# A streaming encoder layer: part of the last residual moved to GpSimd, and one chunk's inputs loaded at another place

## The chip, the cores and the metric

The kernel runs on one core of a Trainium2 chip. The metric is device time in microseconds (us) of one execution; the kernel before took 3009.01 us (median of 3 runs, 3008.19 to 3012.99). The core's engines have queues of their own: TensorE (PE in the profile; its weight loads are PEld), VectorE (DVE), ScalarE (ACT), GpSimd (POOL) and SyncE (SP), which here only issues transfers (DMA). ScalarE issues the output transfers.

## The reference

One layer of a hybrid encoder, on 2048 prompt tokens and 64 sample tokens of width 1024, in float32:

```
h  = rms_norm(x, g1) * (1 + sc1) + sh1
z  = h @ w_in                       # conv pair | q | k | v | two gates
conv_out = conv_module(...);  attn_out = band_attention(q, k, v) @ w_attn_out
merged = sigmoid(g_conv) * conv_out + sigmoid(g_attn) * attn_out
x  = x + gt1 * (merged @ w_o)
h2 = rms_norm(x, g2) * (1 + sc2) + sh2
gate, up = split(h2 @ w_ffn_in)
y  = x + gt2 * ((silu(gate) * up) @ w_ffn_out)
```

What matters here is the last line, x + gt2 * (...), and the step that makes `merged`.

## The kernel before

The first phase makes the normalised input, the projections, the convolution and the attention, and leaves their results in device memory: c_d (convolution), o_d (attention), g_d (gates). The second phase goes over the tokens in three blocks (CBLOCKS: 0 to 576, 576 to 1344, 1344 to 2112), called block one, two and three here; the variable s is 0, 1, 2. Blocks two and three have six tiles of 128 tokens. Each block is done as follows.

**Merge and output projection.** A block has two chunks of tokens. For each chunk, `merge` (line 1641) goes over eight column tiles (ct): weights from w_conv_out and w_attn_out (key "ca"), products `ps<-cin` with the chunk's inputs, which `load_mixed` (line 1090) brings with four transfers, two of c_d and two of o_d; VectorE applies the gate columns (tile tg, `gate_columns`, line 1084), and the sum is split into a high and a low part m. The input tiles of the first chunk and of the second lie in different buffers (tags half0, four buffers, and half1, ten buffers, which other tiles share). Then come the products with w_o (pw), the residual, and the second norm.

**Feed-forward.** `up` makes gate and up products for 22 feature tiles f (ps), and `down` and `down_pair` multiply the hidden tiles with w_ffn_out (pd) and add the results to a sum per token tile, acc. In blocks two and three the last two feature tiles (20, 21) are done by one last call of `down` (line 2049): for each token tile 12 products, into two PSUM banks (one for each half of 512 columns, of a tag with four banks), and then on VectorE for each half: add acc to the products (line 2084), scale with the gate row gt2 (line 2090), add the residual x1 (line 2091). For the very last tile of the program (`final`), the scale and the residual are applied to acc ahead of the products (lines 2059 to 2063), so that afterwards only the products are scaled and acc added. Ahead of that last call, lines 2148 to 2157 load the last two weight slabs, the gate row (gt), the residual rows x1s (x<-x_d, two transfers a tile), and, for the block that follows, two gate columns and the inputs of both chunks.

**Weights.** The class Weights loads each weight slab into a staging buffer (wst, three of them; wup, wfo), and `split` (line 442) turns it into a high part (whi, on ScalarE) and a low part (wlo, on GpSimd or VectorE). At most five slabs are split ahead. Line 459 gives "ca" slabs to GpSimd; line 460 gives one to VectorE instead when, by the planner's own costs, GpSimd's work stands more than BEHIND = 4000 ns beyond TensorE's. These costs are written in `Stream.add` (line 171); one for GpSimd is 60 + 2.25 ns per element. The planner (Stream) adds up such costs as the program is written and runs pending actions, such as freeing a slab and splitting the next, when TensorE's sum has advanced by 500 ns (`spend`, line 200).

**Order.** What is written in the program is not yet the order on an engine. The framework puts the instructions of each engine in order at build time: of those that are ready by its own reckoning, the one written first goes first. So an instruction can be issued far ahead of its written place: the scaling of the last tile's acc (`acc<-acc,gt`) is written behind the fifth tile's work and ran at 2971.20 us, when the first tile's last products had not begun. `tc.issue_after(ins)` keeps what is written inside it behind ins on that engine. All engine instructions carry line 105 in the profile (the recording helper); the transfers carry their own lines: 1095 is load_mixed, 1087 gate_columns, 383 weights, 2154 the residual rows, 2094 the outputs.

Of the kernel before, what the change touches and what calls it, by code (L numbers as in the profile page):

```python
# [8 lines left out]
F32 = mybir.dt.float32  # L9
# [11 lines left out]
T = SEQ + SMP  # L21
# [232 lines left out]
class Weights:  # L254
# [5 lines left out]
    def __init__(self, tc, engines, pool, dram, stream, keys, source, staging, held, kept):  # L260
        self.tc, self.stream = tc, stream
        self.sync, self.act, self.dve, self.gps = engines
        self.pool, self.dram, self.keys, self.source = pool, dram, keys, source
        self.staging, self.held = staging, held
        self.sum_pool, self.sum_d, self.sums, self.hold, self.landed = None, None, {}, 0, {}
        self.room, self.leaving = {"wst": staging - 2, "wup": 0, "wfo": 0}, {"wst": 0, "wup": 0, "wfo": 0}
        times, raws, self.limit, self.pin = {}, {}, 1 << 30, None
        self.wait = True
        self.items, self.users, self.need, self.first, self.stored = [], [], {}, set(), {}
        self.unsaved = set()  # L270

        def item(key):
            self.items.append(key)
            self.users.append(0)
            return len(self.items) - 1

        self.rows = {}
        for i, key in enumerate(keys):
            n = times[key] = times.get(key, 0) + 1
            if key[0] == "dn" and n == 1:  # L280
                for f in (key[1], key[1] + 1):
                    if f not in self.rows:
                        self.rows[f] = item(("fr", f))
                self.need[i] = [self.rows[f] for f in (key[1], key[1] + 1)]
                for j in self.rows_of(key):
                    self.users[j] += 1
            elif key[0] == "up" and n == 1:
                self.first.add(i)
                cs = [c for f, op in key[1:] for c in self.columns_of(f, op)]
                for c in cs:  # L290
                    if c not in raws:
                        raws[c] = item(("fi", c))
                self.need[i] = sorted({raws[c] for c in cs})
                for f, op in key[1:]:
                    for c in self.parts_of(f, op):
                        self.users[raws[c]] += 1
            elif n == 1 or not kept(key) or n == 2 and key[:2] == ("qkv", 0):
                if n == 1 and key[:2] == ("qkv", 0):
                    self.unsaved.add(i)
                self.need[i] = [item(key)]  # L300
                self.users[self.need[i][0]] += 1
        self.raws = raws
        self.again = {key for key, n in times.items() if n > 1 and kept(key)}
        self.loaded, self.ready, self.used, self.freed, self.given = {}, [], 0, 0, 0

        self.extra = {"wup": 1, "wfo": 2}
        self.tags = {"fo": ("wfo", "wup", "wst"), "": ("wst", "wup")}
        self.due = {kind: [] for kind in self.tags}
        for i, key in enumerate(self.items):
            self.due[self.kind(key)].append(i)  # L310
        self.load_on("")
# [130 lines left out]
    def split(self):  # L442
        i = len(self.ready)
        key = self.keys[i]
        its = self.need.get(i, ())
        if i in self.first:
            shape = [P, 4 * len(key) - 4, P]
        elif key[0] == "dn":
            shape = [P, len(DN[key[2]]), 512]
        else:  # L450
            shape = list(self.loaded[its[0]][0].shape) if its else self.stored[key][1]
        hi = self.pool.tile(shape, F32R, tag="whi", name="whi", bufs=self.held)
        lo = self.pool.tile(shape, F32R, tag="wlo", name="wlo", bufs=self.held)
        self.ready.append((hi, lo))
        if not its:
            for t, d in zip((hi, lo), self.stored[key][0]):
                self.sync.dma_start(t.bitcast(F32), d)
            return
        e, name = (self.dve, "dve") if key[0] in ("in", "qkv") or key[0] == "wo" and key[1] % 2 else (self.gps, "pool")
        if name == "pool" and self.sum_pool and self.stream.load["pool"] - self.stream.load["pe"] > BEHIND:  # L460
            e, name = self.dve, "dve"
        if i in self.first:
            parts = [(slice(4 * j, 4 * j + 4), self.operand(f, op)) for j, (f, op) in enumerate(key[1:])]
            self.stream.after("act", "pool")
        elif key[0] == "dn":
            parts = [(slice(j, j + 1), part) for j, part in enumerate(self.down_parts(key))]
            self.stream.after("act", "pool")
        else:
            n = 4 if key[0] == "fi" else shape[1]
            parts = [(slice(j, j + n), self.loaded[its[0]][0][:, j : j + n]) for j in range(0, shape[1], n)]  # L470
        for c, src in parts:
            self.act.activation(hi[:, c], src, AF.Copy)
            self.stream.after(name, "act")
            with self.tc.issue_after(self.pin.ins) if self.pin is not None and name == "dve" else nullcontext():
                e.tensor_tensor(lo[:, c], src, hi[:, c].bitcast(F32), ALU.subtract)
        if i in self.first:
            its = [self.raws[c] for f, op in key[1:] if op[0] == "a" for c in self.parts_of(f, op)]
        elif key[0] == "dn":
            its = self.rows_of(key)
        for j in its:  # L480
            self.drop(j, name)

        def then():
            if key in self.again and key not in self.stored and i not in self.unsaved:
                ds = [self.dram.tile(shape, F32, name="w_d" + "_".join(map(str, key)) + "_" + part) for part in "hl"]
                for t, d in zip((hi, lo), ds):
                    self.sync.dma_start(d, t.bitcast(F32))
                self.stored[key] = ds, shape
            self.presum()

        self.stream.at(self.stream.when(name), then, True)
# [98 lines left out]
def streaming_layer(ctx: ExitStack, tc: tile.TileContext, I, O):  # L590
# [1050 lines left out]
    def merge(c0, c1, src, m, ahead, load):  # L1641
        n = c1 - c0
        for ct in range(KT):
            g = ahead.pop(0)
            if ct == 2 and load:
                load()
            wh, wl = W.get(("ca", ct))
            ps = [
                columns(
                    kts(wh, 4 * j, 4 * j + 4), kts(wl, 4 * j, 4 * j + 4), kts(src[0][j], 0, 4), kts(src[1][j], 0, 4), 0, n  # L1650
                )[:, :n]
                for j in range(2)
            ]
            t = piece("t1", "t1")[:, :n]
            stream.after("dve", "pe")
            dve.scalar_tensor_tensor(t, g[0][:, :n], 1.0, ps[0], ALU.add, ALU.mult)
            dve.scalar_tensor_tensor(ps[1], g[1][:, :n], 1.0, ps[1], ALU.add, ALU.mult)
            W.done()
            if ct + 2 < KT:
                ahead.append(gate_columns(c0, c1, ct + 2))  # L1660
            dve.scalar_tensor_tensor(ps[1], ps[1], 2.0, t, ALU.mult, ALU.add)
            stream.after("act", "dve")
            if c0:
                split(m[0][:, ct, :n], m[1][:, ct, :n], ps[1])
            else:
                split_sample(m[0][:, ct, SMP : SMP + n], m[0][:, ct, :SMP], m[1][:, ct, :n], ps[1])
# [102 lines left out]
    for s, (lo, hi) in enumerate(CBLOCKS):  # L1769
# [279 lines left out]
        def down(fs, ws):  # L2049

            last = fs[-1] == NF - 1
            for i, (t, n) in enumerate(tiles):
                if fs[0] == 0:
                    acc[i] = token_row("acc")
                pss = [ps_g.tile([P, 512], F32, tag="gp", name="pd", bufs=4) for _ in range(2)]
                gt = gt2[int(t < SMP)] if last else None
                final = last and hi == T and i == len(tiles) - 1
                x1 = [x1s[q // 3][:n, q % 3] for q in (2 * i, 2 * i + 1)] if last else None
                if final:
                    for j in range(2):  # L2060
                        dst = acc[i][:n, 512 * j : 512 * j + 512]
                        dve.tensor_tensor(dst, dst, gt[:n, 512 * j : 512 * j + 512], ALU.mult)
# [9 lines left out]
                for j, ps in enumerate(pss):  # L2072
# [1 line left out]
                    dst = acc[i][:n, f]  # L2074
                    m = 2 * n if n == SMP else n
                    both = acc[i][:m, f]
                    stream.after("dve", "pe")
                    if fs[0] == 0:
                        act.activation(both, ps[:m], AF.Copy)
                    elif not last:  # L2080
# [73 lines left out]
                nc.sync.dma_start(x1s[q // 3][:n, q % 3], x1_d[t : t + n, 512 * j : 512 * j + 512])  # L2154
        if s + 1 < len(CBLOCKS):
            nxt = [gate_columns(*tile_chunks(*CBLOCKS[s + 1])[0], ct) for ct in range(2)]
            srcs = [load_mixed(*c, i) for i, c in enumerate(tile_chunks(*CBLOCKS[s + 1]))]
        down(list(range(end, NF)), ws)
        stream.flush()

# [28 lines left out]
```

## Time and profile before

| | |
|---|---|
| Median of 3 runs | 3009.01 us |
| Profiled execution | 3009.85 us |
| Its span, first to last instruction | 3008.0 us |
| Mean granted TensorE clock | 0.987 |
| TensorE busy | 2919.7 us, 97% |
| VectorE busy | 2029.9 us, 67% |
| GpSimd busy | 915.9 us, 30% |

A row of the timeline gives the start in us from the span's start, the duration (of a merged group, from its first start to its last end), the engine, the line, the operation, out<-in by tile names, the shapes, the count, and in brackets the engine's idle time just before, with what ended it. In a row of windows stand, for each engine, busy us and the number of instructions, then the granted clock, the DMA engines' busy share, and GB/s. The chain of waits follows the work that ended last back through what released it.

### The profile page before, as it was taken

To read this page: it belongs to the slowest core of one execution; us is meant where nothing else is said; L and a number is where in the kernel's file an instruction comes from. 1 tells how busy PE (TensorE), PEld (TensorE's weight loads), DVE (VectorE), ACT (ScalarE), POOL (GpSimd) and SP (SyncE) were. 2 spreads that over 40 slices of the span, in tenths; PEclk is the share of its full clock that TensorE was granted. 3 is DMA by queue.
4 is the path that set the end of the run, shared out by engine and by line. 5 is a ranking of instruction groups with operands and counts; after the bars stand their busy time and mean duration, and the time that the engine had idled before them with its cause. 6 is when DMAs were issued, how large, how long until landed. Compare 5 with 4: busy or idle time off the path is not lost.

```text
span 3008.0 us, 44650 instructions
## 1 busy us (share of the span) xinstructions
PE 2919.7 (97%) x16199; PEld 2603.0 (87%) x16199; DVE 2029.9 (67%) x3671; ACT 1323.1 (44%) x2375; POOL 915.9 (30%) x575
## 2 busy tenths in 40 slices
PE   7999989999999999989999999999999999999998
PEld 4889867888888788888999999999999898999997
DVE  5887676777867885577777756556666657366567
ACT  3334642563356257464444345434444244333332
POOL 1200210011011102345456432256665341333331
PEclk9999999999999999999999999999999999999999
DMA  9788889878988788886444786446556955355544
GB/s 301 258 295 286 274 262 298 290 249 283 301 266 265 262 251 272 267 285 235 153 153 157 269 266 222 144 140 207 197 175 218 335 194 192 119 169 174 168 161 174
DMA packets 487017, 690.95 MB, mean 230 GB/s; under 512 B 38420, under 2 KB 316808, under 8 KB 486797
## 3 DMA queue, kind: packets, MB, share of 16 engines
q1 hardware_dynamic: 469749, 662.07, 66.8%
q10 hardware_dynamic: 17048, 26.04, 2.4%
q8 instruction: 127, 2.08, 0.3%
q14 instruction: 93, 0.76, 0.1%
HBM read 503.79 MB, written 184.19 MB: 229 GB/s over the span
## 4 chain that ended last, share of the span: by engine, by line
PE 84%; DVE 7%; DMA 5%; issue 1%; ACT 1%; POOL 1%; SPq 0%; ACTq 0%; DVEq 0%; POOLq 0%
PE ps L105 55%; PE pd L105 14%; PE pw L105 6%; PE po L105 2%; PE sc L105 2%; DVE y L105 2%; PE ptp L105 2%; PE pt L105 1%; DMA cin<-o_d 1%; DVE wlo L105 1%; PE pa L105 1%; POOL r L105 1%; DVE pr L105 1%; DMA tg<-g_d 0%; DMA x<-x_d 0%
## 5 line engine op out<-in xcount | busy, mean ns | idle before, releaser
L105 POOL TENSOR_TENSOR wlo<-wst,whi 128x1024 fp32r<-128x1024 f32 (+1 forms) x168 | 384.8, 2294 | 562.8 <-ACT whi L105 500.4
L105 PE MATMUL ps<-t,whi 128*128 128x384 f32 (+1 forms) x2112 | 506.9, 323 | 8.5 <-DVE t L105 6.2
L105 PE MATMUL pd<-whi,hid 128*128 128x512 f32 x1356 | 441.2, 391 | 3.4 <-DVE acc L105 3.4
L105 ACT ACTIVATE whi<-wst 128x1024 fp32r<-128x1024 f32 (+1 forms) x271 | 265.0, 982 | 397.4 <-PE ps L105 132.1
L105 PEld LDWEIGHTS ps<-t,whi 128*128 128x128 f32 x2112 | 370.8, 189 | 17.5 <-DVE t L105 7.4
L105 PE MATMUL ps<-b,whi 128*128 128x384 f32 (+1 forms) x1584 | 379.6, 325 | 4.1 <-DVE pt L105 1.7
L105 DVE SCALAR_TENSOR_TENSOR y<-u,wd,y 128x512 f32<-128x512 f32 (+1 forms) x480 | 367.4, 772 | 6.5
L105 PE MATMUL ps<-hh,whi 128*128 128x512 f32 (+2 forms) x992 | 363.9, 367 | 0.0
L105 PE MATMUL ps<-hh,wlo 128*128 128x512 f32 (+2 forms) x992 | 348.7, 351 | 0.0
L105 PE MATMUL ps<-hl,whi 128*128 128x512 f32 (+2 forms) x992 | 348.3, 351 | 0.0
L105 PE MATMUL ps<-t,wlo 128*128 128x384 f32 (+1 forms) x1056 | 340.9, 323 | 0.0
L105 DVE TENSOR_TENSOR acc<-acc,pd 128x512 f32<-128x512 f32 x440 | 289.8, 683 | 65.8 <-PE pd L105 62.3
L105 PEld LDWEIGHTS pd<-whi,hid 128*128 128x128 f32 x1356 | 254.5, 188 | 58.6 <-DVE acc L105 7.0
L105 PEld LDWEIGHTS ps<-b,whi 128*128 128x128 f32 x1584 | 276.9, 189 | 6.2 <-DVE v L105 2.1
L105 PE MATMUL pd<-wlo,hid 128*128 128x512 f32 x700 | 273.8, 391 | 0.0
L105 PE MATMUL ps<-b,wlo 128*128 128x384 f32 (+1 forms) x792 | 256.4, 324 | 0.0
L105 ACT ACTIVATE pr<-pr,sm 128x640 f32<-128x640 f32 (+3 forms) x272 | 200.9, 747 | 120.8 <-DVE sm L105 118.4
L105 PEld LDWEIGHTS ps<-hh,wlo 128*128 128x128 f32 x992 | 189.6, 191 | 22.2 <-DMA wlo<-w_din_l 0.4
L105 PEld LDWEIGHTS ps<-hh,whi 128*128 128x128 f32 x992 | 190.2, 192 | 19.1 <-issue 1.8
L105 PEld LDWEIGHTS ps<-hl,whi 128*128 128x128 f32 x992 | 190.3, 192 | 16.0 <-issue 1.4
L105 PEld LDWEIGHTS ps<-t,wlo 128*128 128x128 f32 x1056 | 199.3, 189 | 0.9
L105 POOL TENSOR_TENSOR r<-t,mhalf 128x1 f32<-128x1 f32 (+3 forms) x68 | 80.6, 1186 | 381.0 <-DVE t L105 378.2
(218 smaller groups left out, 5652.2 us busy)
## 6 DMA issues: line engine op xcount, KB each, us to landing
whi<-w_din_h SPq DMA_DIRECT2D x72, 512.0 KB, 5.2
wlo<-w_din_l SPq DMA_DIRECT2D x72, 512.0 KB, 6.5
wst<-sum_d SPq DMA_DIRECT2D x132, 256.0 KB, 2.9
wmod<-in_w_ada SPq DMA_DIRECT2D x48, 512.0 KB, 6.9
sum_d<-ws SPq DMA_DIRECT2D x88, 256.0 KB, 2.2
wst<-in_w_ffn_in SPq DMA_DIRECT2D x84, 256.0 KB, 3.2
wst<-in_w_in SPq DMA_DIRECT2D x40, 512.0 KB, 7.6
wst<-in_w_ffn_in SPq DMA_DIRECT2D x37, 512.0 KB, 5.5
```

The lines of the kernel that those rows point to most:

```text
L105: return f(*args, **kw)
```

## The change

In the last `down` call of blocks two and three, the sums acc of the third, fourth and fifth of the six tiles are scaled with gt2 and get their residual x1 on GpSimd, behind the last weight split that was given to GpSimd up to there (W.low), and written ahead of the products. After the products of these tiles VectorE then scales the products and adds acc. The other tiles are left as they were. And of the next block's inputs only those of the first chunk are loaded ahead of that `down` call; those of the second chunk are loaded from within the first chunk's merge, at its seventh column tile (block one keeps its load at the third).

```diff
@@ Weights.split
-                e.tensor_tensor(lo[:, c], src, hi[:, c].bitcast(F32), ALU.subtract)
+                low = e.tensor_tensor(lo[:, c], src, hi[:, c].bitcast(F32), ALU.subtract)
+            self.low = low if name == "pool" else self.low
@@ merge
-            if ct == 2 and load:
+            if ct == (6 if c0 else 2) and load:
                 load()
@@ down
             last = fs[-1] == NF - 1
+            ahead = range(len(tiles) - 4, len(tiles) - 1) if last and s else ()
+            with tc.issue_after(W.low.ins) if ahead else nullcontext():
+                for i, j in [(i, j) for i in ahead for j in range(2)]:
+                    dst = acc[i][:, 512 * j : 512 * j + 512]
+                    gps.tensor_tensor(dst, dst, gt2[0][:, 512 * j : 512 * j + 512], ALU.mult)
+                    gps.tensor_tensor(dst, dst, x1s[(2 * i + j) // 3][:, (2 * i + j) % 3], ALU.add)
...
-                final = last and hi == T and i == len(tiles) - 1
+                final = last and (i in ahead or hi == T and i == len(tiles) - 1)
...
-                if final:
+                if final and i not in ahead:
                     for j in range(2):
...
-                    stream.after("dve", "pe")
+                    stream.after("dve", "pe", *["pool"] * (i in ahead))
@@ ahead of the last down call
-            srcs = [load_mixed(*c, i) for i, c in enumerate(tile_chunks(*CBLOCKS[s + 1]))]
+            srcs = [load_mixed(*tile_chunks(*CBLOCKS[s + 1])[0], 0)]
         down(list(range(end, NF)), ws)
```

More of the change, by code (lines that the diff above doesn't have):

```diff
@@ L266, in __init__ @@
         self.room, self.leaving = {"wst": staging - 2, "wup": 0, "wfo": 0}, {"wst": 0, "wup": 0, "wfo": 0}
-        times, raws, self.limit, self.pin = {}, {}, 1 << 30, None
+        times, raws, self.limit, self.pin, self.low = {}, {}, 1 << 30, None, None
         self.wait = True
```

## The prediction

> **What bounds the kernel now.** I read the page's busy shares and chain first, then the timeline of each engine around the two places that the diff touches: the last down-projection products of a block, and the start of the next block's merge.
>
> ```profile
> PE 2919.7 (97%) x16199; PEld 2603.0 (87%) x16199; DVE 2029.9 (67%) x3671; ACT 1323.1 (44%) x2375; POOL 915.9 (30%) x575
> PE 84%; DVE 7%; DMA 5%; issue 1%; ACT 1%; POOL 1%; SPq 0%; ACTq 0%; DVEq 0%; POOLq 0%
> ```
>
> TensorE is busy nearly everywhere, so only places where it stands still, and the end of the program, can give time. The timeline of block three's end shows VectorE, then a TensorE row that waited:
>
> ```profile
> 2986.99 1.29 DVE L105 TENSOR_TENSOR pd<-pd,acc 128x512 f32<-128x512 f32 x2
> ...
> 2989.39 1.27 DVE L105 TENSOR_TENSOR acc<-pd,x 128x512 f32<-128x512 f32 x2
> 2990.58 1.29 DVE L105 TENSOR_TENSOR pd<-pd,acc 128x512 f32<-128x512 f32 x2
> ...
> 3003.74 1.27 DVE L105 TENSOR_TENSOR acc<-pd,acc 128x512 f32<-128x512 f32 x2
> 2990.12 0.50 PE L105 MATMUL pd<-whi,hid 128*128 128x512 f32 x1 [0.55 <-DVE acc L105]
> ```
>
> VectorE has no gap. A tile is six instructions, started 0.60 us apart: 3.59 us from 2986.99 to 2990.58. TensorE waits for it each time, because each tile needs two of four PSUM banks and the banks come back only with VectorE's last add. The end of the program is VectorE's at 3005.01, and the last output transfer closes the span of 3008.0. Block two has the same shape, and its last wait is the first product of the next merge:
>
> ```profile
> 2344.71 1.38 DVE L105 TENSOR_TENSOR pd<-pd,acc 128x512 f32<-128x512 f32 x2
> 2365.13 1.27 DVE L105 TENSOR_TENSOR acc<-pd,x 128x512 f32<-128x512 f32 x2
> 2362.28 0.62 PE L105 MATMUL ps<-cin,whi 128*128 128x384 f32 x2 [0.55 <-DVE acc L105]
> ```
>
> After it, the chain of waits through the boundary of blocks two and three, the TensorE row at its end, and the windows of the merge products (busy, count, granted clock, DMA share, GB/s):
>
> ```profile
> 2355.51 14.82 DMA cin<-o_d
> 2370.82 4.80 DMA wst<-in_w_attn_out
> 2375.72 0.75 ACT whi L105
> 2376.69 0.48 ACT m L105
> 2377.19 0.57 DVE m L105
> 2377.80 0.62 PE L105 MATMUL ps<-cin,whi 128*128 128x384 f32 x2 [2.55 <-DVE m L105]
> 2362.28:2374.92 12.64, 12.64 (x71) 12.64 (x72) 1.00 1.00 340
> 2374.92:2384.00 9.08, 6.50 (x27) 5.67 (x27) 0.81 1.05 339
> ```
>
> Inputs of the second chunk (cin) stand in SyncE's queue ahead of merge weights; ScalarE has to wait for the weights with the split of m behind it; m's split holds a PSUM bank; TensorE stops. It made 27 products in 9.08 us, where at the earlier pace (12.64 / 71 = 0.178 us) they take 4.8: this place costs 4.3 us, partly idle, partly at a granted clock of 0.81.
>
> **The change, part by part. Block three's tail.** Removed from VectorE: for tiles three to five, the scale and the residual add drop out of the sequence add, scale, add residual for each half; what stays is scale the products, add the sum. That is 2 instructions x 3 tiles = 6, at 0.60 us: 3.6 us, if VectorE goes on setting the pace. TensorE's tile is 2.85 us (2990.12 until its bank wait), VectorE's new tile 4 x 0.60 = 2.39. Followed through: VectorE ends tile three at 2992.97, four at 2995.4, five at 2997.8; TensorE, unstalled, ends tile six near 2998.6, and VectorE needs its second half at 2999.5. So TensorE doesn't take over, and the end moves from 3005.0 to 3001.4. The other bound: where the halves arrive one after another, the two instructions of a half run dependent, 0.74 us apart, as in block one's tail:
>
> ```profile
> 1724.70 0.70 DVE L105 TENSOR_TENSOR pd<-pd,gt 128x512 f32<-128x512 f32 x1
> 1725.43 0.69 DVE L105 TENSOR_TENSOR acc<-pd,x 128x512 f32<-128x512 f32 x1
> ```
>
> Then a tile is 2.94 and the gain 3 x (3.59 - 2.94) = 1.9 us. I take 3.3, near the interleaved end, which is what this stage shows.
>
> **The work added to GpSimd** is 12 instructions per block of a form that the trace has with other operands; its groups:
>
> ```profile
> L105 POOL TENSOR_TENSOR ws<-wfo,ws 128x512 f32<-128x512 f32 x16 | 20.8, 1302 | 4.7 <-DVE x L105 4.0 <-POOL ws L105 0.2
> L105 POOL TENSOR_TENSOR ws<-ws,wup 128x512 f32<-128x512 f32 x8 | 14.4, 1800 | 0.6
> ```
>
> 1.30 us each, 1.80 at worst: 15.6 us a block (21.6). Does it end before VectorE asks? In block three GpSimd is free from 2962.25, the gate row lands at 2971.2, and the second half of tile three gets its last sum late:
>
> ```profile
> 2960.97 1.28 POOL L105 TENSOR_TENSOR wlo<-wst,whi 128x512 fp32r<-128x512 f32 x1 [1.28 <-ACT whi L105]
> 2971.20 1.29 DVE L105 TENSOR_TENSOR acc<-acc,gt 128x512 f32<-128x512 f32 x2 [1.82 <-DMA gt<-gt_d]
> 2981.31 1.27 DVE L105 TENSOR_TENSOR acc<-acc,pd 128x512 f32<-128x512 f32 x2
> ```
>
> Even if GpSimd stands in order at that sum until 2982.6, its ten remaining instructions end at 2995.6, and VectorE wants the last at about 2997.2. Covered by 1.6 us; were it late, VectorE's whole queue, tile six included, would stand behind it.
>
> **Block two's tail.** GpSimd first has weight splits, behind the last of which the new work is ordered:
>
> ```profile
> 2339.52 7.15 POOL L105 TENSOR_TENSOR wlo<-wst,whi 128x1024 fp32r<-128x1024 f32 x3 [11.08 <-DMA x<-x_d]
> 2343.47 0.68 DVE L105 TENSOR_TENSOR acc<-acc,pd 128x512 f32<-128x512 f32 x1
> ```
>
> The third of these splits is written inside the last down call (its buffer comes free only with the last paired product), so after the new work. The planner then has GpSimd 12 x (60 + 2.25 x 512) ns = 14.5 us ahead, over its limit BEHIND of 4 us (line 460), and gives that split to VectorE. So GpSimd starts the new work near 2344.3 and ends by 2360, in time for tile five (adds near 2359 to 2361); but VectorE, which bounds this stage, gets a 128x1024 split that it didn't have:
>
> ```profile
> 2389.45 1.22 DVE L105 TENSOR_TENSOR wlo<-wst,whi 128x1024 fp32r<-128x1024 f32 x1
> 2378.73 2.32 DVE L105 TENSOR_TENSOR wlo<-wst,whi 128x1024 fp32r<-128x1024 f32 x1
> 2375.28 4.68 POOL L105 TENSOR_TENSOR wlo<-wst,whi 128x1024 fp32r<-128x1024 f32 x2 [10.30 <-ACT whi L105]
> ```
>
> 1.22 us alone, 2.32 beside a busy GpSimd. For the first product of the merge the removed instructions of two tiles count (2.4 us, tile three and four; after that TensorE's own 2.85 a tile is the pace): gain 2.4 - 1.2 to 2.4 - 2.3 = 1.2 to 0.1; I take 0.6. Bounds: 2.4 if the split stays on GpSimd, and a loss if GpSimd runs late (below).
>
> On that price, the Trainium skill (SBUF — State Buffer, "SBUF: two separate sides") says that a VectorE instruction with two SBUF inputs and a GpSimd instruction that reads SBUF lock each other out, whichever starts first finishing undisturbed. The row of 2.32 us agrees: it began under the GpSimd pair, which ended at 2379.96, and ran on 1.1 us after that. By the rule alone the split costs 1.22 plus at most one GpSimd instruction, 2.5 us, and block two's gain would be nothing; the instructions that have a PSUM operand would not be touched.
>
> **The moved loads.** Four transfers at each of two boundaries leave their place before the last down call and are written at the seventh column tile of the merge:
>
> ```profile
> 2348.30 1.03 SPq L1095 DMA_DIRECT2D cin<-o_d  x2
> 2351.68 1.08 SPq L1095 DMA_DIRECT2D cin<-c_d  x2
> 2355.51 4.92 SPq L1095 DMA_DIRECT2D cin<-o_d  x2
> 2363.84 0.37 SPq L383 DMA_DIRECT2D wst<-in_w_conv_out  x1
> 2362.74:2366.33 3.59, 3.59 (x22) 3.59 (x22) 3.59 (x8) 0.00 (x0) 2.24 (x1) 1.00 1.06 402
> cin<-o_d SPq DMA_DIRECT2D x4, 768.0 KB, 12.3
> ```
>
> The four from 2351.68 on are those of the second chunk: 3.07 MB, 7.7 us at 402 GB/s. The buffer of the waiting weights came free with the first split (2341.9). Without the four, the weights can go out near 2350 and land before 2363; the last of them landed at 2375.6. The stall of 4.3 us goes; next late are the gate columns, two buffers deep, so I take 4.0. Bounds: 0 and 4.3. The moved transfers are not needed before the second chunk:
>
> ```profile
> 2434.42 0.51 PE L105 MATMUL ps<-cin,whi 128*128 128x384 f32 x2
> ```
>
> Issued at their written place, near 2391, plus the 14.8 us that the slowest took, they land at 2406, 28 us early. At the boundary of blocks one and two the same queue costs little:
>
> ```profile
> 1735.64 0.19 PEld L105 LDWEIGHTS ps<-cin,wlo 128*128 128x128 f32 x1 [0.49 <-POOL wlo L105]
> 1750.76 0.30 PEld L105 LDWEIGHTS ps<-cin,whi 128*128 128x128 f32 x2 [0.68 <-DVE m L105]
> ```
>
> Bounds 0 and 1.2; I take 0.5.
>
> On the stall's size, the Trainium skill (TensorE: Matmul & The Clock Gate, "Part 1") says that the clock falls after an idle window of about 3.4 us. Here it was 0.81 after 2.55 us of idleness. By the rule only the idle part, some 2.6 us, would come back; the row decides for 4.3.
>
> **Sum:** 3.3 + 0.6 + 4.0 + 0.5 = 8.4 us. The profiled execution took 3009.85 us (span 3008.0), so 3001.4 by it; the median of the runs is 3009.01, 0.84 less, which would give 3000.6. I say 3001.0.
>
> **Rivals.** *The loads don't get out of the way.* The program's order is not the issue order: the framework issues what is ready.
>
> ```profile
> 2322.36 0.45 SPq L1095 DMA_DIRECT2D cin<-c_d  x1
> ```
>
> This one, of the first chunk, went out 20 us before its written place. The second chunk's buffers come free at 2340, the weights' at 2341.9; if that order decides, the queue stays as it was and only the tails gain: 3.9, 3005.5. Against it: the transfers that are written earlier go first while the queue is full (share 1.06).
>
> *The stall only moves* to the gate columns or the next weights and half of it stays: 3.9 + 2.2, 3003.3. For it: boundary one already has small waits of this kind.
>
> *GpSimd makes VectorE wait, and it is slower.* If the third split stays ahead on GpSimd, block two's new work starts at 2346.7; at 1.80 us each it ends at 2368.3, VectorE's add of tile five follows, and the first merge product comes near 2369, 6.7 us late. Block three: 2982.6 + 10 x 1.80 = 3000.6, plus 0.7 and tile six's 3.6: no gain. With the stall covered (4.3) and 0.5, the sum is +1.9: 3011.3. It decides from 1.5 us per instruction on. Against it: 1.30 is the mean of most groups, and VectorE's instructions here read PSUM.
>
> *Everything at its good end:* 3.6 + 2.4 + 4.3 + 1.2 = 11.5, 2997.9.
>
> **How the numbers follow.** Forecast 0.56, loads in the way 0.24, stall moves 0.07, GpSimd late 0.06, all good 0.07. This kernel's measurement tells 0.2% (6.0 us) from nothing, so faster is below 3003.0 and slower above 3015.0. Faster: nearly all of the forecast, all good and a little of the moved stall, 0.62. Same: loads in the way and the rests, 0.33. Slower: GpSimd late at its worst, 0.05. The range goes from 2996.5 (just past all good) to 3006.5 (past the loads in the way).
>
> **What would show it.** Block three: from the first down product of the tail to VectorE's last instruction 3.3 us less than before, with four instructions in tiles three to five. Block two: one 128x1024 split on VectorE inside the tail; TensorE waits for the sum shrink. Boundary: weights issued ahead of the second chunk's cin, the granted clock at 1.00 through the merge, no 2.5 us gap. Wrong if cin still stands ahead of the weights, or if VectorE's adds of tiles three to five wait for GpSimd.

## The result, and the profile after

The changed kernel took 3002.89 us (median of nine runs, 2999.85 to 3006.80), the kernel before 3009.92 us in the same comparison (nine runs, 3008.19 to 3016.30). The ratio is 0.9974, 95% interval [0.9966, 0.9983]: 5 to 10 us less. A second comparison gave 0.9973 [0.9963, 0.9983]. The forecast of 3001.0 us was 1.9 us too low and its range held the time.

The profiled execution took 2999.85 us, span 2998.1: the fastest of the nine. Its page, busy time by engine and the chain's shares by engine:

```profile
PE 2914.3 (97%) x16199; PEld 2600.2 (87%) x16199; DVE 2028.5 (68%) x3661; ACT 1323.5 (44%) x2375; POOL 943.0 (31%) x597
PE 83%; DVE 7%; DMA 4%; POOL 2%; issue 2%; ACT 1%; SPq 0%; ACTq 0%; DVEq 0%; POOLq 0%
```

Nothing in these shares says where the 9.9 us between the two spans went; they are read at four places. In the changed kernel's rows load_mixed carries line 1096 and gate_columns 1088, one higher than before. The timeline of the changed kernel at the end of block three (start, duration, engine, operation):

```profile
2965.72 2.40 DVE L105 TENSOR_TENSOR acc<-acc,gt 128x512 f32<-128x512 f32 x2 [2.68 <-DMA gt<-gt_d]
2965.76 7.26 POOL L105 TENSOR_TENSOR acc<-acc,gt 128x512 f32<-128x512 f32 x5 [9.85 <-DMA gt<-gt_d]
...
2972.48 0.56 DVE L105 TENSOR_TENSOR hid<-ps,hid 128x384 fp32r<-128x384 f32 x1 [0.56 <-ACT hid L105]
...
2980.10 3.77 POOL L105 TENSOR_TENSOR acc<-acc,x 128x512 f32<-128x512 f32 x3
2983.77 0.50 PE L105 MATMUL pd<-whi,hid 128*128 128x512 f32 x1 [0.55 <-DVE acc L105]
2984.23 1.29 DVE L105 TENSOR_TENSOR pd<-pd,gt 128x512 f32<-128x512 f32 x2
2985.42 1.28 DVE L105 TENSOR_TENSOR acc<-pd,acc 128x512 f32<-128x512 f32 x2
...
2993.80 1.28 DVE L105 TENSOR_TENSOR acc<-pd,acc 128x512 f32<-128x512 f32 x2
```

The same stretch of the kernel before began with this row:

```profile
2978.84 0.56 DVE L105 TENSOR_TENSOR hid<-ps,hid 128x384 fp32r<-128x384 f32 x1 [0.56 <-ACT hid L105]
```

From the first write of the last pair's hidden tile (2972.48) to VectorE's last instruction (2995.08) it is 22.60 us; before, the same stretch was 26.17 (2978.84 to 3005.01). Tiles three to five now have four VectorE instructions each. GpSimd is through with its sums at 2983.87, before VectorE takes the first of them at 2985.42. From the first tile's products on VectorE still has no gap: it bounds this tail as before, only with six instructions fewer.

The timeline of the changed kernel at the end of block two:

```profile
2338.83 0.56 DVE L105 TENSOR_TENSOR hid<-ps,hid 128x384 fp32r<-128x384 f32 x1 [0.56 <-ACT hid L105]
...
2342.86 4.76 POOL L105 TENSOR_TENSOR acc<-acc,gt 128x512 f32<-128x512 f32 x3
2343.26 1.97 DVE L105 TENSOR_TENSOR wlo<-wst,whi 128x1024 fp32r<-128x1024 f32 x1
...
2352.56 6.30 POOL L105 TENSOR_TENSOR acc<-acc,x 128x512 f32<-128x512 f32 x5
2358.91 0.68 DVE L105 TENSOR_TENSOR acc<-pd,acc 128x512 f32<-128x512 f32 x1
2348.28 0.50 PE L105 MATMUL pd<-whi,hid 128*128 128x512 f32 x1 [1.61 <-DVE acc L105]
2351.86 0.50 PE L105 MATMUL pd<-whi,hid 128*128 128x512 f32 x1 [0.57 <-DVE acc L105]
2360.16 0.52 PE L105 MATMUL ps<-cin,whi 128*128 128x384 f32 x2
```

The kernel before at the same hidden tile:

```profile
2340.23 0.56 DVE L105 TENSOR_TENSOR hid<-ps,hid 128x384 fp32r<-128x384 f32 x1 [0.56 <-ACT hid L105]
```

The third weight split has moved to VectorE, at the head of the tail, and TensorE's first wait for a free bank has grown to 1.61 us. One of 0.57 follows; the later ones are gone, the one ahead of the merge (0.55 before) too. In sum 21.33 us from the hidden tile to the first merge product, 22.05 before (2340.23 to 2362.28). GpSimd's last sum was ready at 2358.86, and VectorE took it at 2358.91: here there was no room to spare.

The timeline of the changed kernel through the boundary of blocks two and three, and its windows there (busy and count for TensorE, its weight loads, VectorE, ScalarE, GpSimd; granted clock, DMA share, GB/s):

```profile
2349.72 0.37 SPq L383 DMA_DIRECT2D wst<-in_w_conv_out  x1
2350.22 0.64 SPq L383 DMA_DIRECT2D wst<-in_w_attn_out  x1
...
2360.54 1.50 SPq L1096 DMA_DIRECT2D cin<-c_d  x2
...
2381.21 0.38 SPq L1096 DMA_DIRECT2D cin<-o_d  x1
2376.22 0.56 DVE L105 SCALAR_TENSOR_TENSOR t<-tg,ps 128x384 f32<-128x384 f32 x1 [3.05 <-DMA tg<-g_d]
2379.56 0.62 PE L105 MATMUL ps<-cin,whi 128*128 128x384 f32 x2 [0.16 <-DVE m L105]
2428.07 0.51 PE L105 MATMUL ps<-cin,whi 128*128 128x384 f32 x2
```

```profile
2360.16:2372.80 12.64, 12.64 (x73) 12.64 (x72) 8.49 (x15) 5.00 (x6) 7.16 (x3) 1.00 1.08 368
2372.80:2384.00 11.20, 11.04 (x63) 10.72 (x62) 6.42 (x12) 4.05 (x5) 2.40 (x1) 1.00 1.04 387
```

The first of the merge weights goes out at 2349.72, 14 us earlier than before (2363.84), and the second chunk's inputs follow behind three pairs of weights. The wait of 2.55 us is gone but for 0.16, the clock stays at 1.00, and from the first merge product to the first product of the second chunk it is 67.91 us, 72.14 before (2362.28 to 2434.42).

What the prediction read as a mean clock of 0.81 is one piece of half clock in the kernel before, right behind the wait; its window:

```profile
2378.40:2381.81 3.41, 3.38 (x12) 2.87 (x11) 3.41 (x4) 1.27 (x2) 1.56 (x1) 0.50 1.02 323
```

Half of 3.41 us is 1.71 us; with the wait of 2.55 us that makes 4.26 (an estimate), the 4.3 us of the stall.

### The profile page after: what moved, and what is told of

It reads as the page before. It is cut to its first block, busy times and chain, and to the rows that moved or that the text cites. A ratio compares the mean times of both kernels' runs of the same rounds, so it can differ in the third digit from the quotient of the medians.

```text
span 2998.1 us, 44671 instructions
## 1 busy us (share of the span) xinstructions
PE 2914.3 (97%) x16199; PEld 2600.2 (87%) x16199; DVE 2028.5 (68%) x3661; ACT 1323.5 (44%) x2375; POOL 943.0 (31%) x597
## 4 chain that ended last, share of the span: by engine, by line
PE 83%; DVE 7%; DMA 4%; POOL 2%; issue 2%; ACT 1%; SPq 0%; ACTq 0%; DVEq 0%; POOLq 0%
PE ps L105 54%; PE pd L105 15%; PE pw L105 6%; DVE y L105 2%; PE sc L105 2%; PE po L105 2%; PE ptp L105 2%; PE pt L105 1%; DVE wlo L105 1%; POOL r L105 1%; PE pa L105 1%; DMA kk<-k_d 1%; DMA whi<-w_din_h 1%; DVE pr L105 1%; DMA bias<-rb_d 0%
```

## The experiments

All kernels are judged by the same four stretches of their profile. "One to two" and "two to three" are the boundaries: from a block's first merge product to the first product of its second chunk. "Tail two" goes from the first hidden tile of the last pair to the next block's first merge product, "tail three" from the first hidden tile of block three's last pair to VectorE's end. Two values are two executions of one kernel. The ratio is that of the timed runs to those of the kernel before in the same comparison.

| kernel | one to two | tail two | two to three | tail three | ratio [95%] |
|---|---|---|---|---|---|
| before | 68.65, 68.68 | 22.05, 22.04 | 72.14, 71.39 | 26.17, 26.17 | 1 |
| changed | 67.50, 67.51 | 21.33, 21.35 | 67.91, 68.26 | 22.60, 22.58 | 0.9974 [0.9966, 0.9983], 0.9973 [0.9963, 0.9983] |
| GpSimd's part alone | 68.82, 71.74 | 21.34, 21.35 | 72.42, 74.29 | 22.59, 22.58 | 0.9998 [0.9986, 1.0009], 1.0002 [0.9993, 1.0012] |
| loads alone | 67.49 | 22.05 | 70.37 | 26.17 | 0.9985 [0.9975, 0.9995] |
| sums in block three only | 69.33 | 22.04 | 67.90 | 22.59 | 0.9969 [0.9958, 0.9981] |
| sums unplanned | 67.49 | 19.63 | 68.93 | 22.59 | 0.9965 [0.9952, 0.9978] |
| loads at the third weight | 70.05 | 21.34 | 67.84 | 22.59 | 0.9975 [0.9965, 0.9986] |
| GpSimd's work doubled | 68.56 | 21.36 | 67.49 | 31.01 | 0.9999 [0.9988, 1.0011] |
| pinned | 68.46, 69.08 | 19.60, 19.61 | 68.93, 71.02 | 22.59, 22.59 | 0.9965 [0.9952, 0.9977], 0.9966 [0.9954, 0.9979] |
| pinned, four tiles | 67.49 | 19.61 | 71.35 | 21.70 | 0.9964 [0.9950, 0.9978] |

The tails repeat to 0.03 us wherever the code is the same. The boundaries don't: up to the tail of block two, the changed kernel and its variants (all but GpSimd's part alone and the loads at the third weight) issue the same instructions in the same order on every engine, and their boundary from one to two still lies anywhere from 67.49 to 69.33. A tail is settled by one profile, a boundary isn't.

Two things account for most of a boundary's extra length: TensorE's waits in it, and whether the clock falls beside them. From two to three the clock fell to 0.50, for 3.41 us each time, in both profiles of the kernel before, in the second of GpSimd's part alone, in the second of the pinned kernel and in pinned with four tiles. The longest wait beside it was 1.78 to 2.98 us. It did not fall in the first profile of GpSimd's part alone, whose waits were 1.42 and 2.98 us. In the ten profiles whose merge weights go out ahead of the second chunk's inputs, the stretch took 67.49 to 71.35 us, 69.0 in the mean; in the four with the inputs ahead, 71.39 to 74.29, 72.6 in the mean.

**GpSimd's part alone.** All eight transfers go back ahead of the last down call.

```diff
-            if ct == (6 if c0 else 2) and load:
+            if ct == 2 and load:
...
-            srcs = [load_mixed(*tile_chunks(*CBLOCKS[s + 1])[0], 0)]
+            srcs = [load_mixed(*c, i) for i, c in enumerate(tile_chunks(*CBLOCKS[s + 1]))]
```

> The GpSimd part alone; both chunks' inputs are loaded at their old place. Theory (two separate gains: VectorE's tails, and the weights' place in SyncE's queue): block three's tail, from the split of the last hidden tile to VectorE's last instruction, is 3.6 us shorter than before, block two's tail gains about 0.7 us, and the gap of about 2.5 us at the fourth column tile of block three's merge, with the granted clock near 0.8, is there again; about 3005.5 us, 4 below before. Rival (the stall went because the third weight split moved to VectorE, not because of the loads): no gap at the fourth column tile, about 3001 us, 8 below before.

The tails came as expected (3.58 and 0.71 us), and the stall stayed. But the time was no better: 3011.36 us beside 3011.94. So it was run again, with the kernel before for a second profile:

> GpSimd's part alone once more: its profile showed 3.58 us less in the tail of block three and 0.71 less in that of block two, while its time showed only 0.6 us (ratio 0.9998, to 0.9986 at best). Theory: the two tails are worth their 4.3 us in every execution, the stall at the boundary is of before's size (72 us for the stretch), and the ratio comes out at 0.998 to 0.9995. Rival: the gain of the tails is real, but with the loads where they were the boundary or the stages ahead of it take it back: the ratio stays at 0.9995 or more, and the profile shows a longer stretch (over 73 us from merge to second chunk) or a longer stage elsewhere.

> A second profile of the kernel before. Theory: the stall at the boundary into block three is there in each execution, 71 to 73 us for the stretch from the first merge product to the first product of the second chunk, with TensorE waits of 2 to 4.5 us for m. Rival: it varies by several us from execution to execution, and the 72.14 of the first profile was a long one: 68 to 70 us here.

The kernel before showed its stall again (71.39 us, 2.02 us of waiting for m). GpSimd's part alone took 3013.24 us, ratio 1.0002: not the expected gain, but what its rival said. The second profile shows part of why: the stretch from merge to second chunk is 74.29 us. Its timeline and a window there:

```profile
2364.59 3.96 SPq L1096 DMA_DIRECT2D cin<-o_d  x2
2372.96 0.37 SPq L383 DMA_DIRECT2D wst<-in_w_conv_out  x1
2381.19 1.06 ACT L105 ACTIVATE whi<-wst 128x1024 fp32r<-128x1024 f32 x1 [12.05 <-DMA wst<-in_w_attn_out]
2383.27 0.62 PE L105 MATMUL ps<-cin,whi 128*128 128x384 f32 x2 [1.84 <-DVE m L105]
2388.64 0.69 PE L105 MATMUL ps<-cin,whi 128*128 128x384 f32 x1 [2.98 <-DVE m L105]
```

```profile
2380.00:2392.00 12.00, 7.18 (x32) 6.53 (x31) 7.89 (x11) 5.48 (x7) 4.71 (x2) 0.86 0.90 273
```

The weights still stand behind the inputs (SyncE issues the first at 2372.96), ScalarE waits 12.05 us for them, and TensorE stands still twice. The time to the second chunk is set by when the weights land, so TensorE, which comes to the merge 0.7 us sooner, waits longer: tail two and boundary together are 93.76 and 95.64 us, before 94.19 and 93.43. The gain in block two is thus not seen in the sum. Block three's 3.58 us are in both profiles; yet the second interval leaves out a gain of more than 2 us. In the second of these executions time also went into stretches whose order of instructions is that of the kernel before: 1730.40 us up to block two's first merge product (1726.99 in the first, 1726.48 and 1728.97 before), and one to two at 71.74. From block two's first merge product to VectorE's end the two took 1275.40 and 1280.01 us, the kernel before 1278.54 and 1277.26. In this part, ahead of the last tail, the clock fell to 0.50 for 3.41 us twice and four times, in the kernel before twice and once. With 1.71 us taken off for each, this part would be 2.8 us shorter than the kernel before's in the mean (an estimate). Whether the rest, and the clock's falls, are scatter or a cost that goes with this kernel, two profiles don't settle; it stays open.

**The loads alone.**

```diff
-            ahead = range(len(tiles) - 4, len(tiles) - 1) if last and s else ()
+            ahead = ()
```

> The moved loads alone; all tails on VectorE as before. Theory: 4 to 5 us less than before, all at the two boundaries (about 1.1 from the first merge product of block two to its second chunk, 4.2 in block three); tails as before, VectorE's last instruction 3.6 us later after the last hidden tile than in the changed kernel; about 3004.5 us. Rival (the gains aren't separate: VectorE's late end of tile six in block two holds the merge's banks anyway): under 2 us less than before, about 3008 us.

The ratio is 0.9985, 4.5 us less [1.5, 7.5]. The tails are those of the kernel before, so all of it comes from the boundaries. From two to three its profile shows 70.37 us:

```profile
2377.95 0.62 PE L105 MATMUL ps<-cin,whi 128*128 128x384 f32 x2 [1.60 <-DVE m L105]
2380.99 0.62 PE L105 MATMUL ps<-cin,whi 128*128 128x384 f32 x2 [0.66 <-DVE m L105]
2366.95 8.81 ACTq L2101 DMA_DIRECT2D out<-acc  x3
2375.87 1.06 ACT L105 ACTIVATE whi<-wst 128x1024 fp32r<-128x1024 f32 x1 [8.87 <-DMA cin<-c_d]
```

That is 1.8 us less than the kernel before, not the expected 4.2. The weights stood ahead here too (SyncE issued the first three pairs from 2353.23 to 2361.44). What ScalarE's split stood behind were three output transfers that ScalarE issues itself; the profile puts their wait down to earlier transfers.

**The sums in block three only.** This differs from the loads alone only in block three's tail.

```diff
-            ahead = range(len(tiles) - 4, len(tiles) - 1) if last and s else ()
+            ahead = range(len(tiles) - 4, len(tiles) - 1) if last and s == 2 else ()
```

> The changed kernel with the GpSimd part in block three only. Theory: block two's tail is as before, the first merge product of block three 0.7 us later against the last hidden tile than in the changed kernel; block three's tail still 3.6 us shorter; no gap at the fourth column tile; about 0.7 us above the changed kernel. Rival (block two's part also carries the gain at the boundary): 3 to 5 us above the changed kernel, with the gap back.

Here the boundary took 67.90 us, without a wait for m. Up to there it is the same order of instructions as in the loads alone, so the 70.37 there was one execution's, and the boundary's gain does not need GpSimd's part in block two. The ratio 0.9969 beside 0.9985 for the loads alone puts block three's tail at 4.8 us (4.0 by the medians), which agrees with the 3.58 of the profile: with the loads out of the way this tail counts. How much of it, the times don't tell, since the two intervals overlap.

**The sums unplanned.** The twelve instructions go to the engine past the planner's books, so that line 460 leaves the third split on GpSimd. In the profile they carry their own lines (2057 and 2058) instead of 105.

```diff
-                    gps.tensor_tensor(dst, dst, gt2[0][:, 512 * j : 512 * j + 512], ALU.mult)
-                    gps.tensor_tensor(dst, dst, x1s[(2 * i + j) // 3][:, (2 * i + j) % 3], ALU.add)
+                    nc.gpsimd.tensor_tensor(dst, dst, gt2[0][:, 512 * j : 512 * j + 512], ALU.mult)
+                    nc.gpsimd.tensor_tensor(dst, dst, x1s[(2 * i + j) // 3][:, (2 * i + j) % 3], ALU.add)
```

> The changed kernel, with the new GpSimd instructions left out of the planner's costs, so that the third weight split of block two's tail stays on GpSimd. Theory (that split on VectorE, 1.97 us, eats most of block two's gain): the first merge product of block three comes 1.2 to 2.0 us earlier against the last hidden tile, nothing else moves by more than 0.5 us; 1 to 2 us less than the changed kernel. Rival (the split was no loss, TensorE is the limit of block two's tail, or GpSimd ends later and VectorE waits): same as the changed kernel within 0.5 us, with VectorE waiting for GpSimd at tile five.

Tail two fell to 19.63 us, 2.42 below the kernel before: what the sums alone are worth there. The split on VectorE therefore costs 21.33 - 19.63 = 1.70 us of it. But GpSimd did make VectorE wait. The timeline:

```profile
2358.14 2.45 POOL L105 TENSOR_TENSOR wlo<-wst,whi 128x1024 fp32r<-128x1024 f32 x1
2360.49 1.33 POOL L2058 TENSOR_TENSOR acc<-acc,x 128x512 f32<-128x512 f32 x1
2361.86 0.69 DVE L105 TENSOR_TENSOR acc<-pd,acc 128x512 f32<-128x512 f32 x1 [2.37 <-POOL acc L2058]
2362.60 0.62 PE L105 MATMUL ps<-cin,whi 128*128 128x384 f32 x2 [0.32 <-DVE acc L105]
2365.59 0.62 PE L105 MATMUL ps<-cin,whi 128*128 128x384 f32 x2 [0.61 <-DVE acc L105]
```

The split slid in ahead of the last residual addition; VectorE stood 2.37 us for that one sum, and TensorE felt 0.93 us of it in the merge (0.32 + 0.61). The ratio, 0.9965, is lower than the changed kernel's 0.9974, with intervals that overlap.

**Pinned.** The same, with later GpSimd splits ordered behind the last sum.

```diff
...
+            behind = self.pin if name == "dve" else self.tail
-            with self.tc.issue_after(self.pin.ins) if self.pin is not None and name == "dve" else nullcontext():
+            with self.tc.issue_after(behind.ins) if behind is not None else nullcontext():
...
-                    nc.gpsimd.tensor_tensor(dst, dst, x1s[(2 * i + j) // 3][:, (2 * i + j) % 3], ALU.add)
+                    W.tail = nc.gpsimd.tensor_tensor(dst, dst, x1s[(2 * i + j) // 3][:, (2 * i + j) % 3], ALU.add)
```

> The twelve sums leave the planner's books and the weight splits that GpSimd issues afterwards stand behind the last of them. Theory: in the kernel without planning, the third weight split slid in ahead of the last residual addition and held VectorE for 2.37 us, which TensorE felt as 0.32 + 0.61 us in the stage that follows; behind the additions it starts 1.3 us later at most, nobody waits for it, and the stage goes back to the changed kernel's 67.9 us while the tail of block two keeps its 19.6 us. In all some 2.6 us under the changed kernel's 67.9 + 21.3, so 0.9 us under the kernel without planning. Rival: the split is the next late: the weights of the merge come 1.3 us later, TensorE waits for a wlo tile for 0.5 to 1.5 us, and nothing is gained on the kernel without planning.

> The pinned kernel once more, since five runs of it left its ratio between 0.9952 and 0.9977. Theory: the tail of block two at 19.6 us again against the changed kernel's 21.3, the boundary into block three between 67.9 and 69 us; median 2999 to 3003 us, ratio 0.996 to 0.997, at or just under the changed kernel's 0.9973. Rival: the low median was a small sample, and the ratio comes out above 0.9973.

> The changed kernel again, beside the variants below. Theory: its gain at the boundary from block two to block three belongs to the order of SyncE's transfers, so the stretch from the first merge product of block three to the first product of its second chunk is again 67.9 us (67.4 to 68.9; before 72.14), and the stretch of the boundary from block one to two is 67.5 us (67.0 to 68.5). Rival: the 67.91 was one lucky execution, and the loads alone are worth what the kernel with the loads alone showed, 70.4 us. Median 3001 to 3004 us, ratio to before 0.9965 to 0.9985.

The changed kernel came out as expected at both boundaries (67.51 and 68.26 us); its median, 3004.14 us, is 0.1 above the expected range. In the pinned kernel the waits for acc in the merge were gone, tail two stayed at 19.6 us, and the split was not the next late. The gate columns were. The second pinned execution:

```profile
2380.24 0.55 DVE L105 SCALAR_TENSOR_TENSOR t<-tg,ps 128x384 f32<-128x384 f32 x1 [4.60 <-DMA tg<-g_d]
2380.94 0.75 PE L105 MATMUL ps<-cin,whi 128*128 128x384 f32 x2 [1.78 <-DVE t L105]
```

Behind this wait the clock fell to 0.50 for 3.41 us. The boundary took 68.93 and 71.02 us, not the expected 67.9 and 67.9 to 69; tail two and boundary together are 88.53 and 90.63 us, in the changed kernel 89.24 and 89.61. So in the profiles the 1.7 us go back to the gate columns, in part or whole. The timed ratios, 0.9965 and 0.9966 (3002.11 us in the second comparison), are lower than the changed kernel's 0.9973 and 0.9974 by some 2.4 us, with intervals that overlap: a better kernel is likely but not shown.

**The loads at the third weight**, in all blocks.

```diff
-            if ct == (6 if c0 else 2) and load:
+            if ct == 2 and load:
```

> The second chunk's four loads are asked for at the third weight in all three blocks, not at the seventh in blocks two and three. SyncE's order then has them ahead of the fourth pair of merge weights at the boundary from block one to two, and at the one from two to three almost where the change has them (two of the four pieces some gate loads earlier, all behind the merge weights). Theory (what counts is that the merge weights stand ahead of the loads, not the written place): the boundary into block three stays at 67.9 us (67.4 to 69), the one into block two gives back part of its 1.15 us and stands at 67.5 to 68.7; the kernel is within 2 us of the changed one. Rival (the written place, four weights later, carries the gain): 70 to 72 us in the boundary into block three, and 3 to 4 us above the changed kernel.

From two to three it was 67.84 us, the changed kernel's value: there SyncE's order has the inputs where the change has them, but for two pieces that go some gate loads earlier. From one to two all four inputs now go ahead of the sixth pair of weights in the trace (which the expectation calls the fourth), and that stretch took 70.05 us, with three waits of TensorE of 0.47 to 0.70 us; more than I expected, but one execution. The time is the changed kernel's (3004.21 beside 3004.14 us). The written place showed no value of its own where the order on the queue stayed.

**GpSimd's work doubled** in block three.

```diff
+                    if s == 2:
+                        gps.tensor_tensor(dst, dst, x1s[(2 * i + j) // 3][:, (2 * i + j) % 3], ALU.subtract)
+                        gps.tensor_tensor(dst, dst, x1s[(2 * i + j) // 3][:, (2 * i + j) % 3], ALU.add)
```

> In block three alone each of the six sums on GpSimd is followed by a subtraction and an addition of the same residual, so GpSimd has 24 instructions of 1.28 us, 30.7 us from about 2966, where VectorE asks for the first of its sums at about 2985.4 and for the last at about 2990. Rival of the forecast put to the test (GpSimd makes VectorE wait): GpSimd ends near 2997, VectorE waits 4 to 8 us for the last of its sums, and the end comes 4 to 8 us later than in the changed kernel, so that the gain of the tail (3.57 us) is gone. If VectorE does not wait, the margin is larger than the 3 us that I read between GpSimd's end (2983.9) and VectorE's first use.

```profile
2992.02 13.72 POOL L105 TENSOR_TENSOR acc<-acc,x 128x512 f32<-128x512 f32 x11
2999.47 0.69 DVE L105 TENSOR_TENSOR acc<-pd,acc 128x512 f32<-128x512 f32 x1 [6.80 <-POOL acc L105]
3005.77 0.69 DVE L105 TENSOR_TENSOR acc<-pd,acc 128x512 f32<-128x512 f32 x1 [1.31 <-POOL acc L105]
```

VectorE waits 8.11 us, just past the expected 4 to 8; the tail is 8.41 us longer than the changed kernel's, and the time is back at the kernel before: 3012.81 beside 3012.33 us. Twelve instructions more (15.2 us at 1.27) made 8.1 us of waiting, so the cover was about 7 us.

**Pinned, with a fourth tile** in block three.

```diff
-            ahead = range(len(tiles) - 4, len(tiles) - 1) if last and s else ()
+            ahead = range(len(tiles) - (5 if s == 2 else 4), len(tiles) - 1) if last and s else ()
```

> The pinned kernel with a fourth tile (the second) summed ahead by GpSimd in block three. Theory: VectorE's tail there is one row of operations from 2977 to 2995 without a gap, three behind TensorE's last product (2992.2), so two of its 128x512 operations less (1.2 to 1.3 us) come off it, and TensorE's wait of 0.55 us for a free sum goes as well: from the first hid of the last tile pair to VectorE's end 20.8 to 21.4 us instead of 22.6. GpSimd gets 4 instructions more (5.2 us) and ends near 2989, just ahead of VectorE's last use. Rival: GpSimd ends too late for the third or fourth tile, VectorE waits 0.5 to 2 us for acc, and the stretch stays at 22.6 us or more.

The tail is 21.70 us, 0.89 less, of the 1.2 expected: most of the rest is a short wait for GpSimd. TensorE had no wait left in this tail, and its last product began at 2995.98.

```profile
2990.09 0.69 DVE L105 TENSOR_TENSOR acc<-pd,acc 128x512 f32<-128x512 f32 x1 [0.20 <-POOL acc L2059]
2995.98 0.39 PE L105 MATMUL pd<-whi,hid 128*128 128x512 f32 x1
2997.89 1.27 DVE L105 TENSOR_TENSOR acc<-pd,acc 128x512 f32<-128x512 f32 x2
```

GpSimd's cover is used up with four tiles. The boundary from two to three took 71.35 us, with a wait of 2.11 us of TensorE behind the gate columns and the clock at 0.50 after it. The ratio, 0.9964 [0.9950, 0.9978], can't be told from the pinned kernel's.

## Why the prediction was right, point by point

- **Block three's tail:** forecast 3.3 us (1.9 to 3.6), measured 3.57. The interleaved price, six instructions at 0.60 us (3.59), held to the hundredth; the hedge to 3.3 was not needed. VectorE stayed the bound, as followed through.
- **GpSimd's price and cover:** forecast 1.30 us an instruction, measured 1.27 where VectorE did not disturb it and 1.35 in the mean of block three's twelve. The cover was named 1.6 us, with GpSimd standing at the late sum until 2982.6. That was the step that was off: the framework put five scalings and the additions that were ready ahead of it, GpSimd ended at 2983.87, and the doubled kernel shows some 7 us of cover. By that the slower rival needs some 1.9 us an instruction in this block (an estimate: 1.27 and 7 us over twelve), not 1.5. In block two it was the other way round: "in time for tile five" was right by 0.05 us (2358.86 and 2358.91), and that is luck.
- **Block two's tail:** forecast 0.6 us (0.1 to 1.2), measured 0.72. The third split did move to VectorE by line 460; it ran 1.97 us, between the two prices given, and cost 1.70 of the 2.42 us that the sums alone are worth. The lock rule of the Trainium skill (SBUF — State Buffer, "SBUF: two separate sides") was a fair guide: at 1.97 us the split was longer than the 1.22 alone, within its 2.5, and VectorE's pair of scalings ran 2.40 us beside GpSimd's at 2965.7, 1.29 before. The instructions with a PSUM operand kept their 0.60 us.
- **The boundary from two to three:** forecast 4.0 us (0 to 4.3), measured 4.23 in the first pair of profiles, 3.13 in the second. The weights went out near 2350 and the gate columns came next, as named: 3.05 us of waiting on VectorE, 0.16 on TensorE. More than the idle 2.6 us came back, with the clock at 1.00, so the row of 0.81 was the better guide to the stall's size than the idle window of the Trainium skill (TensorE: Matmul & The Clock Gate, "Part 1"), by which only the idle part would have. In the second pair the wait before was 2.02 us and the one after 0.26, with the same 3.41 us of half clock before; over all profiles the two orders are 3.6 us apart, so 4.0 was a little high. The inputs were not issued near 2391 but from 2360.54 to 2381.21, far ahead of their written place; that did no harm, because the weights were ahead of them.
- **The boundary from one to two:** forecast 0.5 us (0 to 1.2), measured 1.15 and 1.17, at the top of its bounds; executions with the same order lie up to 69.33 us. Their nine have a mean of 68.10, 0.6 us under the kernel before: the forecast 0.5 was nearer than this pair.
- **The sum:** 8.4 us forecast, 8.0 by the time given. The four stretches give 9.67 in the first pair of profiles, whose execution of the changed kernel was the fastest of nine, and 8.58 in the second. The timed difference is 7.0 and 8.2 us by the medians, 7.8 and 8.1 by the ratios. So the sum was about right, in executions that scatter by nearly as much as the difference. That the median of the changed kernel fell below the prediction's line for faster, 3003.0, by 0.1 us is luck.
- **The rivals:** the loads got out of the way, so the first fell. But its price was wrong as well: it gave the tails alone 3.9 us, and the kernel with the tails alone gained nothing that could be measured. The parts of the sum were treated as separate; block two's tail is not separate from the boundary behind it, since a stall that ends when a transfer lands takes back what TensorE gains ahead of it. That accounts for the 0.7 us of block two; why block three's 3.6 us don't show in the times of that kernel is open.

## What to carry to other kernels

An operation that VectorE runs between a product and its freed bank can go to an idle engine ahead of the product, and in a stretch where VectorE has no gap each instruction taken off is worth its spacing; but first follow where the planner and the framework will put what stood on that idle engine. Ahead of a stall that ends with a transfer, a faster engine gained nothing here until the transfer itself was moved up: look at what stands before it in its queue, not at the written place. Judge a tail by one profile, a stretch that waits for transfers by several.

## What the runs showed that I had not expected

- The same instructions in the same order took 1725.82 to 1731.50 us up to block two's first merge product in the changed kernel and the variants with its loads: 5.7 us, nearly what the change is worth, from one execution to another.
- A stall of some 2 us can also lower the clock behind it: 0.86 over the 12 us that hold TensorE waits of 1.84 and 2.98 us (0.50 for 3.41 us from 2388.50 on), 1.00 in the 11 us ahead. It doesn't always.
- GpSimd's order did not follow the text: it ran five scalings in one row (7.26 us) before the first residual addition, and the cover was some 7 us, not the 1.6 that I had worked out for the written order.
